# Decays of a two-way state-space scan asked for in four steps between whole tiles, with exponentials held in ScalarE's traced order

## The chip, the cores and the metric

The kernel runs on one core of one Trainium2 chip. The metric is the device time of one execution in microseconds (us), of which the median of several runs is given. The engines are named as in the profile: PE is TensorE's matmuls, PEld its weight loads, DVE is VectorE, ACT is ScalarE, POOL is GpSimd, and SP is SyncE, whose queue issues the kernel's DMA transfers in this stage.

## The reference

One layer of a hybrid network works on 512 latent tokens behind 256 context tokens, each 1024 wide, all in 32-bit floats. One projection of the normalized input feeds a convolution branch (GLU, 31 taps along rows of 64) and a two-way Mamba-2 scan: 32 heads of 64 in 8 groups, a state of 128, chunks of 128 tokens. Both are gated, merged and projected, and an MLP follows. The part that the change is about is the scan's decay inside a chunk:

```python
cum = jnp.cumsum(dts * a.astype(F32).reshape(g, r), axis=2)
xdt = x5 * dts[..., None]
cum_t = jnp.moveaxis(cum, 2, -1)
seg = cum_t[..., :, None] - cum_t[..., None, :]
lower = jnp.tril(jnp.ones((q, q), dtype=bool))
decay = jnp.exp(jnp.where(lower, seg, -jnp.inf))
cb = jnp.einsum('bcqgn,bckgn->bcgqk', cs_, bs)
y_diag = jnp.einsum('bcgrqk,bckgrp->bcqgrp', cb[:, :, :, None] * decay, xdt)
...
y_off = jnp.einsum('bcqgn,bcgrpn,bcqgr->bcqgrp', cs_, h_in, jnp.exp(cum))
return (y_diag + y_off).reshape(b, l, h, p), h_final
```

The scan runs forward and, on the flipped sequence, backward; the two are added.

## The kernel before

**Projections.** Each weight tile comes as fp32 through SP (`raw`, two buffers), is rounded by ACT (`whi`, L115), and DVE takes the rest (`wlo`, L116). PE then does three matmuls for each of eight steps of the contraction, L124 with whi, L125 with whi and the input's low part, L126 with wlo. A B or X tile has a wide part (512 latent tokens) and a narrow one (256 context tokens). A projection needs its own whi and wlo, and they are made one tile ahead.

**The groups.** The time from about 100 to 585 us goes to a loop over the 8 groups. In each round the outputs of group g are computed, and B, C, X0, X1, Z0 and Z1 of group g + 1 are projected. The order of a round is a string, `STEPS` (`STEPS0` for the first round), which the loop reads word by word: a capital B, C, X or Z is a projection, `Gb Ga` the two halves of a GLU tile (Ga is followed by its 31 taps on DVE, L631), `c` makes cb = C'B and the transposes of B (Bk) on PE and copies them on ACT (L503, L510), `x` transposes X (xps), copies it on ACT (xt, L534) and scales it on DVE (xw, L527), `s` makes the chunk states on PE (sps, L546), of which the first is copied by ACT (hst, L552) and the rest added by DVE, and `y0`, `y1` give the outputs of two heads each (L585, L589). cps, bps, xps and sps share three PSUM buffers, so s can be held up by a late copy of xt or of hst. Eviction of a projection is on ACT (L388), its five-tap convolution on DVE (L392), its SiLU on ACT (L402; Z's at L460).

**What sets the order.** PE runs in the order of the string as long as g is under 7. On the other engines a scheduler orders the instructions by the traced order as a priority and by when it expects them ready; each engine then runs its queue strictly in that order.

**The decays.** A head needs two tiles E of 128 x 512, one for each direction. The forward one comes from a ring of 7 buffers, the backward one from a ring of 3. For each: SP fetches a row, broadcast to all partitions (L478); POOL masks one triangle (`affine_select`, L482); ACT takes four exponentials, one for each chunk (L485). DVE adds both (L487) and, in y, multiplies the sum by cb (L575). A backward buffer comes free with the add. All this stands in `expo(upto)`, which traces all four steps for two heads at once, behind the products of each y and two heads ahead of the need (`LEAD` 2). The other rows from the same source, `Cd` (L571), are multiplied by C on POOL or DVE (L572).

Of the kernel before, what the change touches and what calls it, by code (L numbers as in the profile page):

```python
# [27 lines left out]

STEPS0 = 'Gb Ga c0 B x0 C s X0 y0 X1 y1 c Z0 Z1 x'
STEPS = 'B s Gb C X0 y0 Ga X1 y1 c Z0 Z1 x'


CDB, EB, LEAD, ADDV, E_LATER, E_LATER0 = 7, 7, 2, 1, 0, 0


V_N1, V_N2, V_FN = 0, 8, 16
# [28 lines left out]
def build(tc, xT, ctxT, cond, crow, wada1, wada2, vecs, hv, cst, w_in, w_co, w_so, w_o, w_1, w_2, outT):  # L67
    nc = tc.nc
    with ExitStack() as es:
# [393 lines left out]
        def bc(ap, shape):  # L463
            return ap.unsqueeze(len(shape) - 1).broadcast_to(shape)

        ahead = []
        asked = [0]

        def expo(upto):

            while asked[0] < min(upto, HEADS):
                h = asked[0]
                asked[0] += 1
                es_ = []
                for d in range(2):
                    hd = d * HEADS + h
                    e = (tp if d else spool).tile([P, T], F32, name="E", tag="M" if d else "E", bufs=3 if d else EB)
                    nc.sync.dma_start(e, s_cf[hd, 0].unsqueeze(0).broadcast_to([P, T]))  # L478

                    x3 = e.rearrange("p (c q) -> p c q", q=P)  # L480
                    sign = -1 if d else 1
                    nc.gpsimd.affine_select(x3, x3, pattern=[[0, NCH], [sign, P]], compare_op=ALU.is_ge,  # L482
                                            fill=never, base=0, channel_multiplier=-sign)
                    for c in range(NCH):
                        nc.scalar.activation(x3[:, c], x3[:, c], AF.Exp, bias=bT[:, c, hd:hd + 1])  # L485
                    es_.append(e)
                (nc.vector if ADDV else nc.gpsimd).tensor_tensor(es_[0], es_[0], es_[1], ALU.add)  # L487
                ahead.append(es_[0])

        ch = lambda t, c: t[:, c * P:(c + 1) * P]  # L490
        wi = [lambda c: c if c < 3 else c - 1, lambda c: c - 1]
# [70 lines left out]
        def ssd_y(q, j):  # L562
# [4 lines left out]
            for r in range(2):  # L567
                for d in range(2):
                    hd = d * HEADS + 4 * g + 2 * j + r
                    Cd = (spool if d else tp).tile([P, T], F32, name="Cd", tag="Cd", bufs=CDB if d else 3)  # L570
                    nc.sync.dma_start(Cd, s_cf[hd, 1].unsqueeze(0).broadcast_to([P, T]))  # L571
                    (nc.vector if (d, r) in DECAYS_V else nc.gpsimd).tensor_tensor(Cd, Ct, Cd, ALU.mult)  # L572
                    Cs[d].append(Cd)
                M = ahead.pop(0)
                nc.vector.tensor_tensor(M, M, cb, ALU.mult)  # L575
                Ms.append(M)
            with later(E_LATER):
                expo(4 * g + 2 * j + 2 + LEAD)
# [61 lines left out]
        cur = group(0)  # L640
        proj(cur, "Z0")
        proj(cur, "Z1")
        with later(E_LATER0):
            expo(2 + LEAD)
        begun_glu = 0
        for g in range(G):
            nxt = group(g + 1)
            glu_q = None
            for part in STEPS0.split() if g == 0 else STEPS.split():
# [4 lines left out]
                elif part in ("c", "x"):  # L654
                    if g + 1 < G:
                        (ssd_c if part == "c" else ssd_x)(nxt)
                elif part in ("c0", "x0"):
                    (ssd_c if part == "c0" else ssd_x)(cur)
                elif part == "s":
                    ssd_s(cur)  # L660
                elif part[0] == "y":
                    ssd_y(cur, int(part[1]))
                elif part == "Gb":
                    if begun_glu < NGLU:
                        glu_q = glu_b(begun_glu, spool, "sg")
# [290 lines left out]
```

## Time and profile before

| | |
|---|---|
| median of three runs | 1251.92 us (1250.16 to 1253.42) |
| the profiled execution | 1256.71 us |
| its span on the core | 1254.9 us |
| mean granted clock of PE | 0.984 |
| E tiles: rows, masks, exponentials, adds | 64, 64, 256, 32 |
| ACT: mean exponential of 128 x 128 | 394 ns |
| DVE: mean GLU tap | 719 ns |

How to read it: a profile is of one execution, and its own time stands beside its span. A row of a timeline or of a group of instructions has the start or the share, the engine and line, the operation and its tiles (out<-in), and in brackets how long the engine had stood idle ahead of it and who released it. Each engine works its queue in order, so an instruction that waits holds all behind it. Ahead of the groups lie the conditioning and the input's normalization (to about 100 us); behind them three more GLU tiles, the gates, both output projections and the MLP.

### The profile page before, as it was taken

Reading aid. Unit: us, or ns where it says so; the run is one execution under the profiler, and the core shown is the slowest. Engines: PE = TensorE matmul, PEld = TensorE weight load, DVE = VectorE, ACT = ScalarE, POOL = GpSimd, SP = SyncE. Lnnn points to the kernel's source line nnn. Section 1 sums busy time; section 2 is a strip of 40 time slices with the busy share of each in tenths; the row PEclk is TensorE's granted clock in tenths of the full one; section 3 lists DMA queues with packets and bytes.
Section 4 is the critical chain, followed back from the end, with each engine's and each line's share of the span. In section 5 each row is a group of like instructions: output and inputs, shape, how many; then the busy total and the mean of one; then the engine's idle time right before and its main releaser. Section 6 shows DMA issues by size and latency. Waiting matters only on the chain.

```text
span 1254.9 us, 17442 instructions
## 1 busy us (share of the span) xinstructions
PE 1203.4 (96%) x6662; PEld 1005.0 (80%) x6662; DVE 914.7 (73%) x1426; ACT 598.4 (48%) x941; POOL 156.7 (12%) x138
## 2 busy tenths in 40 slices
PE   6998899999999989999999999999999999999997
PEld 3787778878787878887887878778988888888886
DVE  6797899988989799875999698786843443443454
ACT  4567786847557475842452561134531331332342
POOL 0003523323050314130010000000000000000000
PEclk8999899999999999999999999999999999999998
DMA  9427544425352434333353368855113223323332
GB/s 362 142 61 200 176 138 143 147 79 170 96 190 73 155 113 142 108 118 110 102 186 115 126 201 274 309 164 160 54 56 101 89 96 101 100 86 101 101 101 68
DMA packets 65332, 169.83 MB, mean 135 GB/s; under 512 B 7648, under 2 KB 10464, under 8 KB 65120
## 3 DMA queue, kind: packets, MB, share of 16 engines
q1 hardware_dynamic: 65248, 168.72, 42.3%
q8 instruction: 52, 0.85, 0.3%
q14 instruction: 32, 0.26, 0.1%
HBM read 162.14 MB, written 6.55 MB: 134 GB/s over the span
## 4 chain that ended last, share of the span: by engine, by line
PE 48%; DVE 6%; DMA 6%; ACT 2%; issue 1%; SPq 0%; POOL 0%; DVEq 0%; ACTq 0%; POOLq 0%
PE ps L125 15%; PE ps L126 15%; PE ps L124 15%; DMA aw<-in_wada_dram 2%; DVE conv L631 1%; DVE wlo L116 1%; DMA yr<-s_y 1%; PE yps L589 1%; DMA raw<-in_w_dram 1%; DVE aw L755 1%; DMA raw<-in_w_co_dram 1%; DVE yl L694 1%; DMA raw<-in_w_o_dram 1%; PE sps L546 1%; ACT whi L115 0%
## 5 line engine op out<-in xcount | busy, mean ns | idle before, releaser
L115 ACT CAST whi<-raw 128x1024 fp32r<-128x1024 f32 x163 | 170.9, 1049 | 333.2 <-PE ps L125 314.2
L116 DVE TENSOR_TENSOR wlo<-raw,whi 128x1024 fp32r<-128x1024 f32 x163 | 202.1, 1241 | 105.1 <-ACT whi L115 96.8
L126 PE MATMUL ps<-hh,wlo 128*128 128x512 f32 x632 | 248.5, 393 | 7.8 <-DVE wlo L116 7.8
L124 PE MATMUL ps<-hh,whi 128*128 128x512 f32 x632 | 252.8, 400 | 0.6 <-DVE Bt L392 0.4
L125 PE MATMUL ps<-hl,whi 128*128 128x512 f32 x632 | 247.9, 392 | 0.0
L631 DVE SCALAR_TENSOR_TENSOR conv<-sg,V,conv 128x392 f32<-128x392 f32 (+14 forms) x240 | 168.6, 719 | 2.6
L126 PEld LDWEIGHTS ps<-hh,wlo 128*128 128x128 f32 x632 | 119.3, 189 | 35.7 <-DVE wlo L116 10.3
L124 PEld LDWEIGHTS ps<-hh,whi 128*128 128x128 f32 x632 | 120.0, 190 | 27.0 <-issue 2.4
L125 PEld LDWEIGHTS ps<-hl,whi 128*128 128x128 f32 x632 | 119.8, 189 | 24.8 <-issue 0.6
L791 DVE SCALAR_TENSOR_TENSOR x<-ps,mod,x 128x512 f32<-128x512 f32 (+1 forms) x48 | 31.7, 661 | 99.5 <-PE ps L126 99.5
L485 ACT ACTIVATE E<-E,bT 128x128 f32<-128x128 f32 x256 | 84.0, 394 | 31.0 <-POOL E L482 30.4
L125 PE MATMUL ps<-h2l,whi 128*128 128x512 f32 (+1 forms) x240 | 89.9, 375 | 0.1
L126 PE MATMUL ps<-h2h,wlo 128*128 128x512 f32 (+1 forms) x240 | 89.8, 375 | 0.0
L124 PE MATMUL ps<-h2h,whi 128*128 128x512 f32 (+1 forms) x240 | 89.4, 375 | 0.0
L125 PE MATMUL ps<-gl,whi 128*128 128x512 f32 x224 | 88.4, 395 | 0.0
L124 PE MATMUL ps<-gh,whi 128*128 128x512 f32 x224 | 88.2, 394 | 0.0
L126 PE MATMUL ps<-gh,wlo 128*128 128x512 f32 x224 | 87.9, 392 | 0.0
L572 POOL TENSOR_TENSOR Cd<-Ct,Cd 128x512 f32<-128x512 f32 x48 | 71.2, 1503 | 96.0 <-ACT Ct L402 49.7
L482 POOL TENSOR_SCALAR_AFFINE_SELECT E<-E 128x512 f32<-128x512 f32 x64 | 51.4, 812 | 251.1 <-DMA E<-s_cf 203.8
L392 DVE SCALAR_TENSOR_TENSOR Xt<-ps,V,Xt 128x255 f32<-128x255 f32 (+3 forms) x128 | 75.3, 608 | 9.1 <-ACT Xt L388 8.3
L546 PE MATMUL sps<-xw,Bk 128*128 128x256 f32 x160 | 42.1, 415 | 12.8 <-ACT hst L552 8.8
L124 PE MATMUL ps<-hc,whi 128*128 128x256 f32 x184 | 52.0, 283 | 1.4 <-DVE Xt L392 1.4
(260 smaller groups left out, 2327.5 us busy)
## 6 DMA issues: line engine op xcount, KB each, us to landing
raw<-in_w_in_dram SPq DMA_DIRECT2D x81, 512.0 KB, 3.7
raw<-in_w_dram SPq DMA_DIRECT2D x64, 512.0 KB, 3.6
E<-s_cf SPq DMA_DIRECT2D x64, 256.0 KB, 4.5
Cd<-s_cf SPq DMA_DIRECT2D x64, 256.0 KB, 4.4
aw<-in_wada_dram SPq DMA_DIRECT2D x64, 256.0 KB, 4.2
ablk<-in_wada_dram SPq DMA_DIRECT2D x16, 512.0 KB, 8.9
raw<-in_w_so_dram SPq DMA_DIRECT2D x16, 512.0 KB, 3.8
s_y<-yt SPq DMA_DIRECT2D x16, 256.0 KB, 3.6
```

The costliest lines, as they stand in the source:

```text
L115: nc.scalar.copy(hi, raw)
L116: nc.vector.tensor_tensor(lo, raw, hi, ALU.subtract)
L124: pe(nc.tensor.matmul(ps, lhsT=whi[:, k, :], rhs=rhi[:, k, t0:t1], start=start and k == 0, stop=False))
L125: pe(nc.tensor.matmul(ps, lhsT=whi[:, k, :], rhs=rlo[:, k, t0:t1], start=False, stop=False))
L126: pe(nc.tensor.matmul(ps, lhsT=wlo[:, k, :], rhs=rhi[:, k, t0:t1], start=False, stop=stop and k == KT - 1))
L392: nc.vector.scalar_tensor_tensor(o[:, lo:hi], ps[:, lo + d:hi + d], vcol(V_SCW + 5 * ch + j), o[:, lo:hi], ALU.mult, ALU.add)
L482: nc.gpsimd.affine_select(x3, x3, pattern=[[0, NCH], [sign, P]], compare_op=ALU.is_ge, fill=never, base=0, channel_multiplier=-sign)
L485: nc.scalar.activation(x3[:, c], x3[:, c], AF.Exp, bias=bT[:, c, hd:hd + 1])
L546: pe(nc.tensor.matmul(ps[:, d * 256:(d + 1) * 256], lhsT=ch(Bk, c), rhs=xw[d][:, wi[d](c)].rearrange("p h e -> p (h e)"), start=i == 0, st ...
L572: (nc.vector if (d, r) in DECAYS_V else nc.gpsimd).tensor_tensor(Cd, Ct, Cd, ALU.mult)
L631: nc.vector.scalar_tensor_tensor(o[:, :, lo:hi], u[:, :, lo + d:hi + d], wv(j), o[:, :, lo:hi], ALU.mult, ALU.add)
L791: nc.vector.scalar_tensor_tensor(x1[:, j, a:b], ps[:, a:b], mod[:, gcol + j, 0:1], x1[:, j, a:b], ALU.mult, ALU.add)
```

## The change

1. `expo` is taken apart into `expo_rows` (SP), `expo_select` (POOL), `expo_exp` (ACT) and `expo_add` (DVE). A word `e` in the string calls `expo()`, which advances one head: the add for the head 2 ahead, the exponentials 3 ahead, the mask 4 ahead, the rows 5 ahead (`LEADS`). A word `E` in the first round primes them (`expo_first`).
2. The first of the four exponentials of each tile is passed to the scheduler's `keep_in_program_order`, which puts it behind the ACT instruction traced just before it.
3. The strings change: four `e` in each round, one between two whole tiles. In the first round C and X0 come ahead of s, and a second GLU tile is done there; in the later rounds both halves of the GLU tile stand together, ahead of X0. Five tiles in all are done in the groups as before: two in round 0 and one each in rounds 1 to 3, in place of one each in rounds 0 to 4.

The diff's core:

```diff
-STEPS0 = 'Gb Ga c0 B x0 C s X0 y0 X1 y1 c Z0 Z1 x'
-STEPS = 'B s Gb C X0 y0 Ga X1 y1 c Z0 Z1 x'
-CDB, EB, LEAD, ADDV, E_LATER, E_LATER0 = 7, 7, 2, 1, 0, 0
+STEPS0 = 'Gb Ga c0 B x0 C X0 s E e X1 e y0 e Gb Ga y1 e c Z0 Z1 x'
+STEPS = 'B s e C e Gb Ga X0 y0 e X1 e y1 c Z0 Z1 x'
+LEADS = (2, 3, 4, 5)
...
+        def after_traced(ins):
+            tc.keep_in_program_order(ins)
...
+        def expo_exp(h):
+            for d in range(2):
+                hd = d * HEADS + h
+                e3 = chain[d][h].rearrange("p (c q) -> p c q", q=P)
+                for c in range(NCH):
+                    i = nc.scalar.activation(e3[:, c], e3[:, c], AF.Exp, bias=bT[:, c, hd:hd + 1])
+                    if c == 0:
+                        after_traced(i)
...
+        def expo_first():
+            for h in range(LEADS[3]):
+                expo_rows(h)
+            for h in range(LEADS[2]):
+                expo_select(h)
+            for h in range(LEADS[1]):
+                expo_exp(h)
+            for h in range(LEADS[0]):
+                expo_add(h)
+
+        def expo():
+            n = step[0]
+            step[0] += 1
+            for lead, f in zip(LEADS, (expo_add, expo_exp, expo_select, expo_rows)):
+                if 0 <= n + lead < HEADS:
+                    f(n + lead)
...
-                M = ahead.pop(0)
+                M = chain[0][4 * g + 2 * j + r]
                 nc.vector.tensor_tensor(M, M, cb, ALU.mult)
                 Ms.append(M)
-            with later(E_LATER):
-                expo(4 * g + 2 * j + 2 + LEAD)
...
-        with later(E_LATER0):
-            expo(2 + LEAD)
...
+                elif part == "e":
+                    expo()
+                elif part == "E":
+                    expo_first()
```

The code grows by 27 lines, so the lines behind it have other numbers in after: cb's copy is L530, Bk's L537, xt's L561, hst's L579, the exponentials L491, the add L497, the product with cb L602, the taps L656.

How the queues move shows at four places. First ACT in the first round, before: from the end of a long run of exponentials (E) to the copies of cb and Bk.

```order
L388 ACTIVATE Bt_1106<-ps_1107,V_72 128x512 [waits PE_49]
L485 ACTIVATE E_962<-E_962,bT_572 128x128
L485 ACTIVATE E_970<-E_970,bT_572 128x128 [waits DMAHW4_49,Pool_49]
L485 ACTIVATE E_970<-E_970,bT_572 128x128 x3
L485 ACTIVATE E_977<-E_977,bT_572 128x128 [waits DMAHW2_49,Pool_49]
L485 ACTIVATE E_977<-E_977,bT_572 128x128
L388 ACTIVATE Bt_1106<-ps_1137,V_72 128x256 [waits PE_49]
L115 CAST whi_1256<-raw_1254 128x1024 [waits DMAHW0_49]
L485 ACTIVATE E_977<-E_977,bT_572 128x128 x2
L503 COPY cb_1087<-cps_1082 128x512
L510 COPY Bk_1089<-bps_1090 128x512
L510 COPY Bk_1089<-bps_1096 128x256
```

The same stretch of ACT after, from the first of these copies on.

```order
L376 COPY bT_572<-dtp_791 128x64
L650 ACTIVATE conv_717<-sg_956,V_72 128x512 [waits DVE_49]
L530 COPY cb_1027<-cps_1022 128x512 [waits PE_49]
L537 COPY Bk_1029<-bps_1030 128x512 [waits PE_49]
L537 COPY Bk_1029<-bps_1036 128x256 [waits PE_49]
L491 ACT_TABLE_LOAD [waits DMAHW5_49,Activation_49]
L491 ACTIVATE E_1262<-E_1262,bT_572 128x128 [waits Pool_49]
L491 ACTIVATE E_1262<-E_1262,bT_572 128x128
L491 ACTIVATE E_1262<-E_1262,bT_572 128x128 [waits Activation_49]
L491 ACTIVATE E_1264<-E_1264,bT_572 128x128 [waits DMAHW6_49,Pool_49]
L491 ACTIVATE E_1264<-E_1264,bT_572 128x128 x3
```

The copies of cb and Bk have moved from behind the exponentials to ahead of all of them.

Second, ACT in the same round after, around the copy hst of the first state (Ct_1140 and Xt_1178 are C and X0 of the next group, whi_1475 is a rounded weight).

```order
L491 ACTIVATE E_1327<-E_1327,bT_572 128x128 [waits DMAHW7_49]
L388 ACTIVATE Xt_1178<-ps_1179,V_72 128x512 [waits PE_49]
L491 ACTIVATE E_1327<-E_1327,bT_572 128x128 x2
L491 ACTIVATE E_1410<-E_1410,bT_572 128x128 [waits DMAHW0_49]
L491 ACTIVATE E_1410<-E_1410,bT_572 128x128
L402 ACT_TABLE_LOAD [waits DVE_49]
L402 ACTIVATE Ct_1140<-Ct_1140 128x512 [waits Activation_49]
L388 ACTIVATE Xt_1178<-ps_1209,V_72 128x256 [waits PE_49]
L115 CAST whi_1475<-raw_1473 128x1024 [waits DMAHW0_49]
L579 COPY hst_1240<-sps_1241 128x512 [waits PE_49]
```

Before, hst stood directly behind the second copy of xt; after, a SiLU with its table load, an eviction and a rounding stand ahead of it.

Third, DVE between rounds 0 and 1, after: the end of the stretch between the wlo of the B projected at the start of round 1 (wlo_1744, seven rows ahead of the first row here) and the add that frees the buffer of E_1844.

```order
L656 SCALAR_TENSOR_TENSOR conv_717<-sg_956,V_72,conv_717 128x8x49 [waits DVE_49]
L554 TENSOR_TENSOR xw0_1716<-xps_1718,wgT_573 128x512 [waits PE_49]
L116 TENSOR_TENSOR wlo_1849<-raw_1846,whi_1848 128x1024 [waits DMAHW6_49,Activation_49]
L554 TENSOR_TENSOR xw1_1717<-xps_1718,wgT_573 128x512
L554 TENSOR_TENSOR xw0_1716<-xps_1725,wgT_573 128x512 [waits PE_49]
L554 TENSOR_TENSOR xw1_1717<-xps_1725,wgT_573 128x256
L554 TENSOR_TENSOR xw0_1716<-xps_1733,wgT_573 128x256 [waits PE_49]
L554 TENSOR_TENSOR xw1_1717<-xps_1733,wgT_573 128x512
L656 SCALAR_TENSOR_TENSOR conv_717<-sg_1504,V_72,conv_717 128x8x54 [waits DVE_49]
L497 TENSOR_TENSOR E_1327<-E_1327,E_1329 128x512 [waits Activation_49]
```

The same place before, from just ahead of the wlo of that B (wlo_1623) on.

```order
L631 SCALAR_TENSOR_TENSOR conv_717<-sg_1016,V_72,conv_717 128x8x61 [waits DVE_49]
L487 TENSOR_TENSOR E_1879<-E_1879,E_1886 128x512 [waits DMAHW5_49,DMAHW1_49,Pool_49]
L631 SCALAR_TENSOR_TENSOR conv_717<-sg_1016,V_72,conv_717 128x8x62 [waits DVE_49]
L116 TENSOR_TENSOR wlo_1623<-raw_1620,whi_1622 128x1024 [waits DMAHW7_49,PE_49,Activation_49]
L631 SCALAR_TENSOR_TENSOR conv_717<-sg_1016,V_72,conv_717 128x8x63 [waits DVE_49]
L575 TENSOR_TENSOR E_1864<-E_1864,cb_1515 128x512
L631 SCALAR_TENSOR_TENSOR conv_717<-sg_1016,V_72,conv_717 128x8x63 [waits DVE_49]
L116 TENSOR_TENSOR wlo_1713<-raw_1710,whi_1712 128x1024 [waits DMAHW2_49,PE_49,Activation_49]
L527 TENSOR_TENSOR xw0_1595<-xps_1597,wgT_573 128x512 [waits PE_49]
L527 TENSOR_TENSOR xw1_1596<-xps_1597,wgT_573 128x512
```

Before, the last add of the round (E_1879) stood ahead of that wlo; after, E_1327's stands behind taps of two GLU tiles and all six scalings xw, and on ACT the first exponential of E_1844 stands ahead of hst:

```order
L561 COPY xt_1715<-xps_1725 128x512 [waits DVE_49,PE_49]
L561 COPY xt_1715<-xps_1733 128x512 [waits DVE_49,PE_49]
L388 ACTIVATE Bt_1747<-ps_1748,V_72 128x512 [waits PE_49]
L491 ACTIVATE E_1844<-E_1844,bT_572 128x128 [waits DMAHW7_49,Pool_49]
L388 ACTIVATE Bt_1747<-ps_1778,V_72 128x256 [waits PE_49]
L115 CAST whi_1901<-raw_1899 128x1024 [waits DMAHW5_49,Activation_49]
L491 ACTIVATE E_1844<-E_1844,bT_572 128x128 x2
L579 COPY hst_1809<-sps_1810 128x512 [waits PE_49]
L491 ACTIVATE E_1469<-E_1469,bT_572 128x128
L491 ACTIVATE E_1844<-E_1844,bT_572 128x128
```

Fourth, ACT at the start of the round that computes group 2's states, before.

```order
L485 ACTIVATE E_3110<-E_3110,bT_572 128x128 [waits Pool_49]
L534 COPY xt_2217<-xps_2227 128x512 [waits DVE_49,PE_49]
L485 ACTIVATE E_3110<-E_3110,bT_572 128x128
L534 COPY xt_2217<-xps_2235 128x512 [waits DVE_49,PE_49]
L485 ACTIVATE E_3110<-E_3110,bT_572 128x128 x2
L388 ACTIVATE Bt_2249<-ps_2250,V_72 128x512 [waits PE_49]
L485 ACTIVATE E_3325<-E_3325,bT_572 128x128 [waits DMAHW2_49,Pool_49]
L388 ACTIVATE Bt_2249<-ps_2280,V_72 128x256 [waits PE_49]
L115 CAST whi_2368<-raw_2366 128x1024 [waits DMAHW0_49,Activation_49]
L485 ACTIVATE E_3325<-E_3325,bT_572 128x128
L552 COPY hst_2311<-sps_2312 128x512 [waits PE_49]
```

The same after.

```order
L561 COPY xt_2338<-xps_2348 128x512 [waits DVE_49,PE_49]
L491 ACTIVATE E_2467<-E_2467,bT_572 128x128 [waits DMAHW7_49,Pool_49]
L561 COPY xt_2338<-xps_2356 128x512 [waits DVE_49,PE_49]
L491 ACTIVATE E_2467<-E_2467,bT_572 128x128 x3
L491 ACTIVATE E_2518<-E_2518,bT_572 128x128 [waits DMAHW2_49]
L388 ACTIVATE Bt_2370<-ps_2371,V_72 128x512 [waits PE_49]
L491 ACTIVATE E_2518<-E_2518,bT_572 128x128 x2
L115 CAST whi_2524<-raw_2522 128x1024 [waits DMAHW0_49,PE_49,Activation_49]
L388 ACTIVATE Bt_2370<-ps_2401,V_72 128x256 [waits PE_49]
L579 COPY hst_2432<-sps_2433 128x512 [waits PE_49]
```

The exponentials that wait for POOL (E_3325 before, E_2467 after) stood between the evictions of B and hst and now stand ahead of the evictions, between the two copies of xt.

More of the change, by code (lines that the diff above doesn't have):

```diff
@@ L27 @@
 NEVER, DT_MIN = -1e30, 1e-18
-STEPS0 = 'Gb Ga c0 B x0 C s X0 y0 X1 y1 c Z0 Z1 x'
-STEPS = 'B s Gb C X0 y0 Ga X1 y1 c Z0 Z1 x'
-CDB, EB, LEAD, ADDV, E_LATER, E_LATER0 = 7, 7, 2, 1, 0, 0
+STEPS0 = 'Gb Ga c0 B x0 C X0 s E e X1 e y0 e Gb Ga y1 e c Z0 Z1 x'
+STEPS = 'B s e C e Gb Ga X0 y0 e X1 e y1 c Z0 Z1 x'
+LEADS = (2, 3, 4, 5)
+CDB, EB = 7, 7
 V_N1, V_N2, V_FN = 0, 8, 16
@@ L464, in bc @@
             return ap.unsqueeze(len(shape) - 1).broadcast_to(shape)
[L466 to L488, printed above, removed]
+        chain = [[None] * HEADS for _ in range(2)]
@@ new lines, in build, with expo_rows, expo_select @@
+        step = [0]
+        def after_traced(ins):
+            tc.keep_in_program_order(ins)
+        def expo_rows(h):
+            for d in range(2):
+                e = (tp if d else spool).tile([P, T], F32, name="E", tag="M" if d else "E", bufs=3 if d else EB)
+                nc.sync.dma_start(e, s_cf[d * HEADS + h, 0].unsqueeze(0).broadcast_to([P, T]))
+                chain[d][h] = e
+        def expo_select(h):
+            for d in range(2):
+                e3 = chain[d][h].rearrange("p (c q) -> p c q", q=P)
+                sign = -1 if d else 1
+                nc.gpsimd.affine_select(e3, e3, pattern=[[0, NCH], [sign, P]], compare_op=ALU.is_ge,
+                                        fill=never, base=0, channel_multiplier=-sign)
@@ new lines, in expo_exp, with expo_add @@
+        def expo_exp(h):
+            for d in range(2):
+                hd = d * HEADS + h
+                e3 = chain[d][h].rearrange("p (c q) -> p c q", q=P)
+                for c in range(NCH):
+                    i = nc.scalar.activation(e3[:, c], e3[:, c], AF.Exp, bias=bT[:, c, hd:hd + 1])
+                    if c == 0:
+                        after_traced(i)
+        def expo_add(h):
+            f, b = chain[0][h], chain[1][h]
+            nc.vector.tensor_tensor(f, f, b, ALU.add)
```

## The prediction

> **What bounds the kernel now.** I read the page's first two parts, then the chain of waits of TensorE (PE), then the windows for the granted clock, and last the timelines of PE and ScalarE (ACT) at the places that those named.
>
> ```profile
> PE 1203.4 (96%) x6662; PEld 1005.0 (80%) x6662; DVE 914.7 (73%) x1426; ACT 598.4 (48%) x941; POOL 156.7 (12%) x138
> PE ps L126 <- DVE wlo L116: 10.5, 9, 2.4
> PE sps L546 <- ACT hst L552: 8.8, 5, 2.5
> PE sps L546 <- ACT xt L534: 4.0, 1, 4.0
> PE xps L522 <- ACT cb L503: 4.0, 1, 4.0
> ```
>
> PE works 1203.4 of 1254.9 us. Its matmuls are the same in number and shape after the change, so only its 51.5 idle us, and what the clock loses, can be won. The four rows (us waited, times, longest) hold 27.3 us of the idle time. Three of them name a copy on ACT, though ACT is busy for only 48%. So ACT is not slow but stands still at the wrong moment:
>
> ```profile
> 104.76 6.84 ACT L485 ACTIVATE E<-E,bT 128x128 f32<-128x128 f32 x23
> 116.19 0.57 ACT L503 COPY cb<-cps 128x512 f32<-128x512 f32 x1
> 129.91 0.40 ACT L485 ACTIVATE E<-E,bT 128x128 f32<-128x128 f32 x1 [3.20 <-POOL E L482]
> 130.21 0.56 ACT L534 COPY xt<-xps 128x512 f32<-128x512 f32 x1
> 253.80 0.40 ACT L485 ACTIVATE E<-E,bT 128x128 f32<-128x128 f32 x1 [4.02 <-POOL E L482]
> 255.79 0.57 ACT L552 COPY hst<-sps 128x512 f32<-128x512 f32 x1
> ```
>
> In group 0 a run of 23 exponentials, and more behind it, stands ahead of cb. At 129.91 and 253.80 one exponential waits 3.20 and 4.02 us for its masked row E, and xt or hst, which PE needs, stands behind it in ACT's queue. What PE then lost:
>
> ```profile
> 116.81 2.82 PE L522 MATMUL xps<-C,Xt 128*128 128x128 f32 x12 [3.95 <-ACT cb L503]
> 130.83 5.88 PE L546 MATMUL sps<-xw,Bk 128*128 128x256 f32 x12 [3.96 <-ACT xt L534]
> 187.34 1.13 PE L546 MATMUL sps<-xw,Bk 128*128 128x256 f32 x4 [1.73 <-ACT hst L552]
> 256.41 2.07 PE L546 MATMUL sps<-xw,Bk 128*128 128x256 f32 x4 [2.45 <-ACT hst L552]
> 314.66 0.50 PE L126 MATMUL ps<-hh,wlo 128*128 128x512 f32 x1 [2.42 <-DVE wlo L116]
> 384.41 0.50 PE L126 MATMUL ps<-hh,wlo 128*128 128x512 f32 x1 [2.09 <-DVE wlo L116]
> 453.25 0.50 PE L126 MATMUL ps<-hh,wlo 128*128 128x512 f32 x1 [1.53 <-DVE wlo L116]
> ```
>
> Four matmuls last 2.07 us behind the gap at 256.41 and 1.13 behind that at 187.34: the clock is cut after some gaps. The windows around the cuts (the seventh entry is the granted clock):
>
> ```profile
> 116.00:120.00 4.00, 3.19 (x15) 3.11 (x16) 4.00 (x8) 3.10 (x7) 0.00 (x0) 0.57 0.69 197
> 129.00:137.00 8.00, 6.14 (x14) 4.48 (x15) 5.51 (x8) 7.09 (x19) 3.81 (x7) 0.57 0.38 120
> 256.00:260.00 4.00, 3.59 (x9) 2.89 (x10) 4.00 (x8) 3.31 (x8) 0.00 (x0) 0.57 0.39 111
> 385.00:390.00 5.00, 5.00 (x16) 3.97 (x15) 5.00 (x10) 3.82 (x7) 0.00 (x0) 0.66 0.65 208
> 467.00:472.00 5.00, 4.63 (x13) 3.71 (x14) 5.00 (x9) 3.35 (x8) 0.00 (x0) 0.66 0.36 105
> ```
>
> Length by what is missing to 1.00: 4 x 0.43 = 1.7, 8 x 0.43 = 3.4, 1.7, 5 x 0.34 = 1.7 and 1.7, together 10.2 us. So the waits that the change can reach cost about 27 + 10 = 37 us.
>
> **The change part by part.** The same decays are computed by the same instructions; what changes is when they are asked for, and the place of two GLU tiles. The one addition is table loads: ACT switches between exponentials and SiLU more often, 97 loads in the order of after against 76.
>
> ```profile
> L485 ACT ACT_TABLE_LOAD x31 | 39.8, 1283 | 22.1 <-DMA E<-s_cf 21.7
> L402 ACT ACT_TABLE_LOAD x19 | 24.4, 1283 | 22.6 <-DVE Xt L392 12.4 <-DVE Bt L392 9.9 <-issue 0.3
> 119.12 1.28 ACT L402 ACT_TABLE_LOAD   x1 [0.90 <-DVE Bt L392]
> 120.42 0.85 ACT L402 ACTIVATE Bt<-Bt 128x768 f32<-128x768 f32 x1
> ```
>
> 21 x 1.283 = 27 us more on ACT. I cost them at nothing: ACT would be busy 625 of 1255 us, and a load before a SiLU passes while ACT waits for DVE anyway (12.4 and 9.9 us in the second row). If that cover fails, each is 1.3 us. [...]
>
> The "hold" binds less than its name. In the order of after only the first of four exponentials of a forward row is pinned behind the instruction traced before it; the backward row's first is pinned behind the forward row's fourth, which is itself free. So 32 of 256 are held, and the others still float to where the scheduler expects them to be ready.
>
> *Group 0.* In after cb and Bk stand ahead of the first exponential, and C and X0 come on PE between the transposes x0 and the states s, so that s doesn't meet an xt just queued. Gone: 3.95 + 3.96 us and the clock of the first two windows, 1.7 + 3.4: 13.0. New: hst now stands last in the row SiLU load, SiLU of Ct, Xt's eviction, whi, hst. These last about 1.28 + 0.85 + 0.55 + 1.05 + 0.57 = 4.3 us from the moment that DVE's Ct is ready, against PE's sixteen matmuls of s ahead of the wait (3.61 us, below) if both start together. Between nothing and 4.3 + 1.7 of clock; I take 3.3 + 1.7, near the upper end, since DVE has 11 more GLU taps in group 0. Net -13.0 + 5.0 = **-8.0 us**.
>
> *Group 1.* Here the change loses. PE's next need is hst after B's projection and sixteen matmuls:
>
> ```profile
> 182.00 3.61 PE L546 MATMUL sps<-xw,Bk 128*128 128x256 f32 x16
> 119.74 0.39 PE L125 MATMUL ps<-hl,whi 128*128 128x512 f32 x1
> 124.75 0.40 PE L126 MATMUL ps<-hh,wlo 128*128 128x512 f32 x1
> 109.83 0.28 PE L124 MATMUL ps<-hc,whi 128*128 128x256 f32 x1
> 112.58 0.28 PE L126 MATMUL ps<-hc,wlo 128*128 128x256 f32 x1
> 309.11 4.36 DVE L631 SCALAR_TENSOR_TENSOR conv<-sg,V,conv 128x440 f32<-128x440 f32 x6
> 313.38 1.22 DVE L116 TENSOR_TENSOR wlo<-raw,whi 128x1024 fp32r<-128x1024 f32 x1
> 315.93 1.28 DVE L527 TENSOR_TENSOR xw<-xps,wgT 128x512 f32<-128x512 f32 x2
> L482 POOL TENSOR_SCALAR_AFFINE_SELECT E<-E 128x512 f32<-128x512 f32 x64 | 51.4, 812 | 251.1 <-DMA E<-s_cf 203.8
> E<-s_cf SPq DMA_DIRECT2D x64, 256.0 KB, 4.5
> ```
>
> A wide matmul comes every 5.01/22 = 0.23 us, a narrow one every 2.75/23 = 0.12, so B takes 24 x (0.23 + 0.12) = 8.4 us, and hst is wanted 8.4 + 3.6 = 12.0 us after B's wlo. On ACT it stands behind the first exponential of E_1844, whose buffer is free only after the add E_1327. That add stands on DVE eight taps, one further wlo and six xw behind B's wlo: 8 x 0.73 + 1.2 + 6 x 0.64 = 10.9 us. Then come the add (0.7), the row's transfer (4.5), the select (0.7 alone, 0.8 on average) and the exponential (0.4): 17.2 us. hst is 17.2 - 12.0 = 5 us late; I take 4.5, since taps and xw overlap a little. That is past every gap that cut the clock, so 1.7 more; before had 1.73. B's wlo itself stands behind seventeen taps of two GLU tiles; before's two wlo waits of over 2 us had six taps ahead. I take 1.3 us, between 0 and 2.4. Net 4.5 + 1.7 - 1.7 + 1.3 = **+5.8 us**.
>
> *Groups 2 to 6, hst.* In after the add that frees the late row's buffer stands ahead of B's wlo, by two taps, a product with cb and the wlo itself. From its start the masked exponential is ready after 0.7 + 4.5 + 0.7 + 0.4 = 6.3 us; B's wlo ends some 4.1 us after that start, and PE then has 8.4 us of B left before s asks for xt, and 12.0 before it asks for hst. So the slack is 4.1 + 8.4 - 6.3 = 6.2 us, and nothing that waits for a row stands between B's evictions and hst. Of the 8.8 - 1.7 = 7.1 us of hst waits in these groups I leave 1.5. Two of the five clock cuts, behind 256.41 and 467, go: 3.4. Net **-9.0 us**.
>
> *Groups 2 to 6, wlo.* Both halves of the GLU tile move ahead of X0, so between the two outputs stands X1 alone, and the products M for y1 no longer heap up ahead of B's wlo beside the taps. The three waits at 314, 384 and 453 are 6.0 us. DVE has as much to do as before, and the row at 314 shows what one late operand costs; I leave 3.5 and the one clock cut (385). Net **-2.5 us**; between -6.0 and +4.
>
> *The rest.* SyncE (SP) issues all rows, Cd loads and weights in one queue, so a row that waits for its buffer holds the weights behind it. A weight load lands in about as long as a row, and both raw buffers are loaded a tile ahead; I cost it at nothing, with +3 as the bound. The stages after the groups keep their order, and their waits are small.
>
> Sum: -8.0 + 5.8 - 9.0 - 2.5 = **-13.7 us**. The profiled run took 1256.71 us (span 1254.9), 4.8 above the median of the three runs, 1251.92. From the profiled run it gives 1243; from the median 1251.9 - 13.7 = **1238.2 us**.
>
> [...]
>
> **The rivals.**
>
> *The late row in every group (slower).* Group 1's chain could be the rule: if the add lands over 6.2 us later than walked, each of groups 2 to 6 waits as group 1 does. Price: six waits of 4.5 + 1.7 = 37.2 us in place of 8.8 + 3.4, with group 0's gain and wlo as it is: 37.2 - 12.2 - 8.0 = +17.0, 1269 us; in half of the groups about +5, 1257. For it: 203.8 us in the row L482 above, POOL's wait for rows. Against it: DVE's order in groups 2 to 6. Chance 0.15.
>
> *The loads on the path (slower).* If all 21 loads stood where PE waits, 21 x 1.283 = 27 less 13.7 is +13, 1265 us; seven, one a group, leave 9.0 - 13.7 = -4.7, 1247. For it: in after a SiLU load stands ahead of hst in group 0. Against it: in the later groups they stand behind hst. Chance 0.05 for the first; the second lies within my range. [...]
>
> *The hold binds too little (no change).* The free exponentials block ACT as before: groups 2 to 6 keep their waits, group 0 gives 8.0 and group 1 takes 5.8: -2.2, 1249.7 us. For it: 32 of 256. Against it: in groups 2 to 6 the blocking one has moved ahead of B's evictions. Chance 0.13.
>
> **How the numbers follow.** My forecast has 0.67. About 0.3%, 3.7 us, is what a measurement of this kernel can tell from no change. The forecast's own range is 1238 -8 (wlo at -6.0, group 0's new wait at nothing) to +11 (wlo at +4, SP at +3, hst in two groups kept), 1230 to 1249. To hold 8 in 10 it takes in the no-change rival and reaches nearly to the late row in half of the groups: 1229 to 1256. Faster: 0.67 and a quarter of the no-change rival, 0.70; same 0.11; slower 0.19.
>
> **What would show it.** Right: PE's waits for cb and xt in group 0 gone, one hst wait of 4 to 5 us in group 1, hst of groups 2 to 6 under 2 us in sum, PE idle near 40 us, Exp loads near 42. Wrong: an hst or xt wait in each group with the exponential ahead of it waiting for POOL (the late row); ACT rows of loads just ahead of hst or whi while PE waits (the loads); wlo over 10 us in sum (DVE's order).

## The result and the profile after

The changed kernel takes 1261.49 us in the median of 8 runs (1256.79 to 1264.44), the kernel before 1252.36 us (8 runs, 1250.16 to 1254.09): a ratio of 1.0073, 95% interval 1.0052 to 1.0093. It is slower by 9 us; I had forecast 13.7 us less. The profiled execution took 1257.76 us, one of the shorter ones, and before's, 1256.71, was longer than those eight, so the two profiles differ by 1 us alone. They have to be compared by stage.

The page of after, then PE's chain of waits (us in total, times, longest):

```profile
PE 1204.4 (96%) x6662; PEld 1005.7 (80%) x6662; DVE 927.4 (74%) x1426; ACT 627.7 (50%) x962; POOL 165.2 (13%) x138
```

```profile
PE sps L573 <- ACT hst L579: 8.2, 2, 5.7
PE ps L124 <- DVE Bt L392: 6.5, 2, 6.1
PE ps L124 <- ACT whi L115: 6.0, 2, 3.1
PE ps L126 <- DVE wlo L116: 5.4, 7, 2.3
```

The waits for cb and xt (8.0 us) are gone, the five for hst have become two, those for wlo have halved from 10.5 to 5.4. PE's idle time, for which I had named 40 us, is 51.6 (1256.0 less 1204.4). In place of the waits that went stand two names that before's list did not have in the groups: Bt, 6.1 us at once, and whi, 6.0 us in two waits. Where on PE's timeline the longest lie:

```profile
124.07 0.77 PE L124 MATMUL ps<-hh,whi 128*128 128x512 f32 x1 [6.08 <-DVE Bt L392]
...
200.36 1.22 PE L573 MATMUL sps<-xw,Bk 128*128 128x256 f32 x2 [5.73 <-ACT hst L579]
...
332.92 0.80 PE L124 MATMUL ps<-hh,whi 128*128 128x512 f32 x1 [3.14 <-ACT whi L115]
```

The granted clock around three of the five, from the windows (the entry behind the five engines); it is 0.57 at 260 to 268 and at 332 to 340 as well:

```profile
120.00:128.00 8.00, 3.69 (x8) 2.53 (x9) 7.90 (x14) 6.92 (x21) 6.95 (x7) 0.57 0.77 241
141.00:145.00 4.00, 4.00 (x12) 3.19 (x11) 4.00 (x6) 3.55 (x10) 4.00 (x3) 0.57 0.34 76
199.00:207.00 8.00, 6.64 (x17) 5.29 (x18) 8.00 (x14) 4.03 (x8) 0.08 (x1) 0.57 0.36 98
```

Four long cuts of 8 us and a short one of 4 (at 141), 0.43 x 36 = 15.5 us, against 10.2 before.

For the sum I take the group stage, from PE's first transposes of dt (L371) to the end of its last output matmul. It lasts 484.3 us in before's profile and 489.3 in after's. PE's idle time in it went from 25.7 to 27.4 us, the clock's loss from 10.2 to 15.4; what is left, work at the full clock, is 448.3 and 446.6. So after's group stage lost 6.8 us to waits and clock and the rest gave 1.8 back. The stage behind the groups was 3.6 us shorter (671.0 and 667.4), which is why the two profiles look alike.

**The wait for Bt.** The first exponentials of after, in ACT's timeline, and the chain of waits at that place (start, length, what was waited for):

```profile
111.57 1.28 ACT L491 ACT_TABLE_LOAD   x1 [7.85 <-DMA E<-s_cf]
...
118.07 0.40 ACT L491 ACTIVATE E<-E,bT 128x128 f32<-128x128 f32 x1 [0.87 <-POOL E L483]
118.37 0.76 ACT L388 ACTIVATE Bt<-ps,V 128x512 f32<-128x512 f32 x1
```

```profile
100.73 14.46 DMA E<-s_cf
```

SP's queue in before, and in after, where the first rows were issued:

```profile
97.18 1.31 SPq L478 DMA_DIRECT2D E<-s_cf  x3
```

```profile
98.41 1.34 SPq L366 DMA_DIRECT2D s_dec<-dec  x3
99.85 1.31 SPq L476 DMA_DIRECT2D E<-s_cf  x3
...
DMA to landing us min/median/max: 3.0/4.2/14.5
```

Before issued its first rows at 97.18 us, ahead of the small transfers of the chunk decays (s_dec). After issued them at 99.85, right behind these, and the third took 14.46 us to land, where the median of all rows is 4.2. ACT, which had been through with cb and Bk, stood idle for 7.85 us, then began on the exponentials, and B's eviction, which PE needed, had to wait for twelve of them.

**The waits for whi.** The end of round 3: DVE's last tap of X1, then ACT:

```profile
323.16 0.47 DVE L392 SCALAR_TENSOR_TENSOR Xt<-ps,V,Xt 128x254 f32<-128x254 f32 x1
325.75 0.40 ACT L491 ACTIVATE E<-E,bT 128x128 f32<-128x128 f32 x1 [1.61 <-POOL E L483]
326.17 1.28 ACT L402 ACT_TABLE_LOAD   x1
...
328.33 1.28 ACT L491 ACT_TABLE_LOAD   x1
329.62 0.40 ACT L491 ACTIVATE E<-E,bT 128x128 f32<-128x128 f32 x1
330.04 1.28 ACT L460 ACT_TABLE_LOAD   x1
...
331.83 1.04 ACT L115 CAST whi<-raw 128x1024 fp32r<-128x1024 f32 x1
```

Three loads of 1.28 us stand ahead of the whi that PE waits for, and two of them are there for one exponential of 0.40 us. But before has the same three loads around one exponential at this place:

```profile
304.12 1.28 ACT L402 ACT_TABLE_LOAD   x1 [2.49 <-DVE Xt L392]
...
306.81 1.28 ACT L485 ACT_TABLE_LOAD   x1
308.10 0.40 ACT L485 ACTIVATE E<-E,bT 128x128 f32<-128x128 f32 x1
308.52 1.28 ACT L460 ACT_TABLE_LOAD   x1
...
310.31 1.04 ACT L115 CAST whi<-raw 128x1024 fp32r<-128x1024 f32 x1
```

So the row of loads is not new. New is what stands ahead of it: X1 was ready at 323.63, yet its SiLU's load began 2.5 us later, behind an exponential that waited 1.61 us for POOL's mask. In before that load began as soon as X1 was ready. From X1's last tap to the end of this whi ACT took 9.2 us in after and 7.3 in before. At the end of round 2 it is the same (X1 ready at 250.76, the load at 253.13, an exponential that waited 1.17 us for POOL between them).

The exponentials of after float apart. ACT's order shows a forward tile in two pieces, three exponentials and, some 40 rows further on, the fourth (E_1262 is head 0's, hst_1240 the copy of the first state):

```
95 L491 ACTIVATE E_1262<-E_1262,bT_572 128x128 [waits Pool_49]
...
97 L491 ACTIVATE E_1262<-E_1262,bT_572 128x128 [waits Activation_49]
...
133 L579 COPY hst_1240<-sps_1241 128x512 [waits PE_49]
134 L491 ACT_TABLE_LOAD
135 L491 ACTIVATE E_1262<-E_1262,bT_572 128x128
```

The priming is traced behind s. The held exponential stays behind it; the three free ones run ahead to where the row is expected. Counted over ACT's order, this is so in all 32 forward tiles of after: the held exponential comes last, and ten or more other ACT instructions lie between the first and the last of the four. In before no tile is spread so far. The exponentials at 252.71 and 325.75, which hold up X1's SiLU, are free ones of such tiles. One late piece makes the whole tile late: the add has to wait for it, and with the add the buffer of a later row.

### The profile page after: what moved, and what is told of

Read it like the earlier page. It is cut to its first block, busy times and chain, and to the rows that moved or that the text cites. A ratio compares the mean times of both kernels' runs of the same rounds, so it can differ in the third digit from the quotient of the medians.

```text
span 1256.0 us, 17441 instructions
## 1 busy us (share of the span) xinstructions
PE 1204.4 (96%) x6662; PEld 1005.7 (80%) x6662; DVE 927.4 (74%) x1426; ACT 627.7 (50%) x962; POOL 165.2 (13%) x138
## 4 chain that ended last, share of the span: by engine, by line
PE 59%; DVE 21%; DMA 9%; ACT 6%; issue 4%; POOL 1%; SPq 1%; DVEq 0%; ACTq 0%; POOLq 0%
PE ps L124 18%; PE ps L126 18%; PE ps L125 18%; DVE conv L656 6%; DVE wlo L116 3%; DMA aw<-in_wada_dram 2%; DMA E<-s_cf 2%; DVE Xt L392 2%; PE sps L573 1%; DMA Cd<-s_cf 1%; DMA yr<-s_y 1%; PE yps L614 1%; ACT whi L115 1%; DVE Bt L392 1%; DMA raw<-in_w_dram 1%
## 5 line engine op out<-in xcount | busy, mean ns | idle before, releaser
L124 PE MATMUL ps<-hh,whi 128*128 128x512 f32 x632 | 255.5, 404 | 12.9 <-DVE Bt L392 6.5
L126 PE MATMUL ps<-hh,wlo 128*128 128x512 f32 x632 | 251.5, 398 | 5.2 <-DVE wlo L116 5.1
L656 DVE SCALAR_TENSOR_TENSOR conv<-sg,V,conv 128x392 f32<-128x392 f32 (+14 forms) x240 | 175.8, 757 | 3.1 <-ACT conv L650 0.7
L491 ACT ACTIVATE E<-E,bT 128x128 f32<-128x128 f32 x256 | 85.6, 394 | 51.8 <-POOL E L483 51.2
L483 POOL TENSOR_SCALAR_AFFINE_SELECT E<-E 128x512 f32<-128x512 f32 x64 | 55.5, 877 | 302.5 <-DMA E<-s_cf 262.7
L392 DVE SCALAR_TENSOR_TENSOR Xt<-ps,V,Xt 128x254 f32<-128x254 f32 (+3 forms) x128 | 74.7, 607 | 11.6 <-ACT Xt L388 11.0
```

The source lines that it names most:

```text
L124: pe(nc.tensor.matmul(ps, lhsT=whi[:, k, :], rhs=rhi[:, k, t0:t1], start=start and k == 0, stop=False))
L126: pe(nc.tensor.matmul(ps, lhsT=wlo[:, k, :], rhs=rhi[:, k, t0:t1], start=False, stop=stop and k == KT - 1))
L392: nc.vector.scalar_tensor_tensor(o[:, lo:hi], ps[:, lo + d:hi + d], vcol(V_SCW + 5 * ch + j), o[:, lo:hi], ALU.mult, ALU.add)
L483: nc.gpsimd.affine_select(e3, e3, pattern=[[0, NCH], [sign, P]], compare_op=ALU.is_ge, fill=never, base=0, channel_multiplier=-sign)
L491: i = nc.scalar.activation(e3[:, c], e3[:, c], AF.Exp, bias=bT[:, c, hd:hd + 1])
L656: nc.vector.scalar_tensor_tensor(o[:, :, lo:hi], u[:, :, lo + d:hi + d], wv(j), o[:, :, lo:hi], ALU.mult, ALU.add)
```

## The experiments

Ratios are to the kernel before, run on the same chip, with the 95% interval; differences between two experiments go by their ratios (0.1% is 1.25 us).

**Rows asked for early.**

```diff
         def expo_first():
-            for h in range(LEADS[3]):
-                expo_rows(h)
...
+        for h in range(LEADS[3]):
+            expo_rows(h)
         begun_glu = 0
```

> After, with only the rows of the first five heads asked for ahead of the loop; masks, exponentials and adds are primed where they were. In after these rows stand on SP behind the four transfers of the chunk decays, the first exponential starts at 111.6 us and PE waits 6.08 us at 124 us for DVE's Bt. Theory A (the late rows cost what after lost in the first round): that wait goes, with some 2 us of clock, so 6 to 9 us less than after's 1261.5, near 1254. Theory B (the table loads of the held exponentials): no change, 1261 +- 2.

Measured: 1260.05 us, 1.0062 (1.0041 to 1.0082). PE's waits:

```profile
PE ps L124 <- ACT whi L115: 8.9, 7, 2.9
PE sps L571 <- ACT hst L577: 8.7, 1, 8.7
```

The wait for Bt went, as theory A said, and the time barely moved: a single wait for hst of 8.71 us at 142 took its place, since ACT then stood for 5.15 and 3.03 us at exponentials whose mask wasn't done. So the late rows made the wait for Bt, but they are not what made after slower: without them the same floating exponentials hold up hst.

**No hold.**

```diff
                     i = nc.scalar.activation(e3[:, c], e3[:, c], AF.Exp, bias=bT[:, c, hd:hd + 1])
-                    if c == 0:
-                        after_traced(i)
```

> After, with no exponential held in the traced order; all else is the same. The order has 72 table loads in place of 97. Theory B (lone held exponentials put three table loads ahead of whi, at the ends of rounds 2 and 3): the waits for whi of 2.89 and 3.14 us, 1.24 us of wlo behind the first and some 6 us of clock go, 1248 to 1252. Theory A: the wait of 6.08 us for Bt stays and so does the time, 1260 +- 2.

Measured: 1266.34 us, 1.0111 (1.0089 to 1.0132), slower than after. Both theories fall.

```profile
PE sps L571 <- ACT hst L577: 17.4, 6, 4.8
...
PE ps L124 <- DVE Bt L392: 6.1, 2, 5.7
```

Without a hold the loads were fewer (72), and hst was waited for in six rounds; at 194.79, 342.24 and 414.73 ACT has an exponential that waits 0.55 to 1.04 us for POOL just ahead of it. So the hold does what the change says, as far as it goes: it takes 9 us of hst waits away.

**Almost no table loads in the groups, after and before.** These two kernels leave out the SiLU of B, C, X and Z.

```diff
-            nc.scalar.activation(o, o, AF.Silu)
+            nc.scalar.activation(o, o, AF.Identity)
...
-                    nc.scalar.activation(z, ps, AF.Silu)
+                    nc.scalar.activation(z, ps, AF.Identity)
```

> After, with the SiLU of B, C, X and Z in the groups left out (an identity stands in its place, so that no table has to be changed there). The order has 15 table loads in place of 97. Theory B: the waits for whi go and the kernel is 8 to 14 us faster than after, 1248 to 1253, and ends no later than before with the same thing left out. Theory A: it gains only what before gains by it and stays some 9 us behind that.

> Before, with the SiLU of B, C, X and Z in the groups left out in the same way; 15 table loads in place of 76. Theory B says that before's loads were mostly covered: 1246 to 1252. If the loads of before stood on the path as well, it gains 5 us or more and the comparison with after has to be made between these two alone.

Measured: after so 1258.22 us, 1.0052 (1.0037 to 1.0067); before so 1244.89, 0.9937 (0.9917 to 0.9956). The loads of before cost 0.6%, 8 us, those of after 0.2%, 3 us, and with nearly all loads gone (15 left in all of each kernel) after is 1.15%, 14 us, behind. So the 21 more loads are not what makes after slower; whi is waited for (5.4 us) without them too, the longest time behind exponentials that wait for POOL:

```profile
PE ps L124 <- ACT whi L115: 5.4, 3, 3.3
```

```profile
452.76 1.86 ACT L491 ACTIVATE E<-E,bT 128x128 f32<-128x128 f32 x6 [3.26 <-POOL E L483]
454.52 1.03 ACT L115 CAST whi<-raw 128x1024 fp32r<-128x1024 f32 x1
```

(The scheduler places instructions anew where no load is due, so this says what loads cost in sum, not at one place.)

**One GLU tile a round.**

```diff
-STEPS0 = 'Gb Ga c0 B x0 C X0 s E e X1 e y0 e Gb Ga y1 e c Z0 Z1 x'
+STEPS0 = 'Gb Ga c0 B x0 C X0 s E e X1 e y0 e y1 e c Z0 Z1 x'
```

> After, with the second GLU tile of the first round taken out, so that rounds 0 to 4 do one GLU tile each as in before. Theory C (two tiles' taps on VectorE hold back the add that frees the late row): the wait of 5.73 us for hst in round 1 falls under 2 us and its half-clock stretch goes, 1252 to 1256. Theory D (the decays asked for one at a time and late are what costs): the waits for whi and wlo of the later rounds stay and round 4 gets one more, 1259 to 1264.

Measured: 1261.08 us, 1.008 (1.0057 to 1.0103). The wait in round 1 was still 5.00 us, and hst was waited for in four later rounds by 1.7 to 2.9. Theory C falls: the taps of the second tile are not what held the row back. (The edit also brings a wait of its own, 4.74 us at 156.71 for Cd, with y1 directly behind y0.)

**The new steps in the old order.**

```diff
-STEPS0 = 'Gb Ga c0 B x0 C X0 s E e X1 e y0 e Gb Ga y1 e c Z0 Z1 x'
-STEPS = 'B s e C e Gb Ga X0 y0 e X1 e y1 c Z0 Z1 x'
+STEPS0 = 'E Gb Ga c0 B x0 C s X0 y0 e e X1 y1 e e c Z0 Z1 x'
+STEPS = 'B s Gb C X0 y0 e e Ga X1 y1 e e c Z0 Z1 x'
```

> After's four functions, leads and hold, in the order of before: priming at the head of the first round, two steps behind each y, GLU halves, C, X0 and s where before has them. 81 table loads. Theory D (steps between whole tiles): with the steps back behind the outputs it is like before, 1248 to 1254. Theory E (the leads themselves, a mask and a row that wait for the add three heads on): hst waits return in every round and it is slower than after, over 1262.

Measured: 1278.85 us, 1.0226 (1.0203 to 1.0249). No rise of hst; one wait of 26.73 us in round 0 and one of 7.44 in round 7:

```profile
179.94 1.34 PE L610 MATMUL yps<-E,xt 128*64 128x128 f32 x10 [26.73 <-DVE E L602]
```

ACT ahead of it:

```profile
175.49 0.62 ACT L659 COPY cacc<-conv 128x512 f32<-128x512 f32 x1 [12.79 <-DVE conv L656]
176.01 0.62 ACT L622 ACTIVATE yacc<-yt 128x512 f32<-128x512 f32 x1
176.64 1.28 ACT L491 ACT_TABLE_LOAD   x1
177.94 0.40 ACT L491 ACTIVATE E<-E,bT 128x128 f32<-128x128 f32 x1
```

The held exponential stands behind yacc, which was traced just ahead of it (in y0), and yacc behind a copy that waits 12.79 us for the GLU tile's taps. The time is over theory E's 1262, but without the hst waits that it named, so this decides between neither. It shows the hold's price: a held instruction inherits the waits of what stands ahead of it, 12.79 us here.

**The new order with the old expo.**

```diff
-STEPS0 = 'Gb Ga c0 B x0 C s X0 y0 X1 y1 c Z0 Z1 x'
-STEPS = 'B s Gb C X0 y0 Ga X1 y1 c Z0 Z1 x'
+STEPS0 = 'Gb Ga c0 B x0 C X0 s X1 y0 Gb Ga y1 c Z0 Z1 x'
+STEPS = 'B s C Gb Ga X0 y0 X1 y1 c Z0 Z1 x'
```

> Before's expo and its lead of two heads, with the orders of after: C and X0 ahead of s in the first round, two GLU tiles in it, both GLU halves ahead of X0 in the later ones. 78 table loads. Theory C (the orders cost it): 1257 or more, with a wait for hst in round 1 of 4 us or more. Theory D (the chain costs it, the orders help): the waits for cb stay, that for xt goes, 1244 to 1250.

Measured: 1260.16 us, 1.007 (1.0049 to 1.009). The order alone costs 9 us, with the exponentials as free as before:

```profile
PE sps L546 <- ACT hst L552: 10.7, 4, 4.6
...
PE ps L124 <- ACT whi L115: 6.8, 4, 3.4
```

Theory C named the wait (hst, 4.62 us in round 0 and 3.42 in round 1, where it said 4 or more), if not its reason. Of theory D the wait for xt went and that for cb stayed, but the time refutes that the order helps. The waits for whi come with the order too: at the end of round 3 here 2.10 us for whi and 2.42 for wlo, though X1's SiLU is not held up (its load begins as X1 is ready). How much of after's whi waits is the order's and how much the free exponential's, no run here parts.

**All four held.**

```diff
                     i = nc.scalar.activation(e3[:, c], e3[:, c], AF.Exp, bias=bT[:, c, hd:hd + 1])
-                    if c == 0:
-                        after_traced(i)
+                    after_traced(i)
```

> After, with all four exponentials of a tile held in the traced order instead of the first. 82 table loads in place of 97. If lone exponentials between two SiLUs cost after its waits for whi, these go and it gains 4 to 8 us, 1253 to 1257. If the held ones stand ahead of evictions until their row is there, waits for Bt and hst come in each round, 1265 or more.

Measured: 1249.16 us, 0.9991 (0.9977 to 1.0005): 0.8%, 10 us less than after by one condition taken out, and level with before. No tile is spread over ten instructions any more.

```profile
PE yps L609 <- DVE E L601: 7.5, 1, 7.5
...
PE sps L572 <- ACT hst L578: 3.4, 2, 3.0
```

The long wait for Bt is gone, those for hst are down to 3.4 us, whi has one of 1.57 left over 0.5 (at the end of round 3, with the same three loads ahead of it). What is left is one wait of 7.5 us, y0 of the first round for its own product: now all primed exponentials stand behind s.

**A second and a third profile of after, a second one of before.** No edit.

> The changed kernel itself, a second profile. Its eight times spread from 1256.8 to 1264.4 and the first profile is of one of the short ones. All theories: the same waits in the first two rounds (Bt near 6, hst near 2.5 and 5.7 us) and at the ends of rounds 2 and 3; in the late stage more waits for wlo than the 4.5 us of idle time there in the first profile.

> The kernel before, a second profile. Its first one, 1256.7 us, lies over all its timed runs. If the group stage varies, it is some 480 us here against 484.3; if the stages around vary, 484 again with a shorter late stage. The waits of the group stage are the same ones: cb and xt near 4 us, hst near 2 in most rounds, wlo near 2 at the ends of rounds 2 to 4.

> The changed kernel, a third profile. The group stage again between 486 and 492 us with the waits for Bt, hst and whi of the first two profiles; a time over 1260 would show which stage makes the long executions long.

Measured: after 1256.07 and 1263.44 us, before 1252.66. The group stage was 486.7 and 494.1 us in after (489.3 in the first profile) and 481.2 in before (484.3). The means are 490.0 and 482.7, 7.3 apart. The stage behind the groups was shorter in all three profiles of after (667.4 to 669.5) than in both of before (671.0 and 671.9), by 2.7 us in the mean, so these five executions differ by 4.4 us in all where the medians differ by 9.1: the loss lies in the group stage, and its whole size is not in the profiles. The longest execution, 1263.44, was long in the group stage (494.1, over the 486 to 492 expected), where the clock cost 17.1 us against 11.9 in the shortest. After had the same waits in all three profiles: Bt 5.6 to 6.1, hst of round 1 4.8 to 5.7, whi 2.8 to 3.1 at the ends of rounds 2 and 3. The stages ahead and behind vary by 1 to 2 us from one execution to the next, in both kernels.

**All held, and primed earlier.** The first of these adds the early rows (the diff of the first experiment) to the kernel with all held; the second moves the priming too:

```diff
-STEPS0 = 'Gb Ga c0 B x0 C X0 s E e X1 e y0 e Gb Ga y1 e c Z0 Z1 x'
+STEPS0 = 'Gb Ga c0 E B x0 C X0 s e X1 e y0 e Gb Ga y1 e c Z0 Z1 x'
```

> All four exponentials held, and the first rows asked for ahead of the loop. With all held, y0 of the first round waits 7.50 us for its product, which starts from rows that land late. Theory F (the rows): that wait falls to 2 us or less and its half-clock stretch with it, 1238 to 1243. Theory G (the held exponentials themselves, which stand behind hst): the wait stays, 1247 to 1251.

> As the last, and the priming (masks, exponentials, adds) moved from behind s to directly behind cb and Bk of the first round. Theory G: the wait of y0 goes, the first exponentials stand in the idle time of ScalarE ahead of B's evictions, 1236 to 1242. Theory F: no better than with the rows alone. If they stand ahead of the evictions too long, a wait for Bt of 3 us or more comes back.

Measured: 1244.24 us, 0.9939 (0.9917 to 0.9961), and 1236.55 us, 0.9883 (0.9855 to 0.9911). The rows alone leave the wait of y0 where it was (8.92 us, so theory G, though the time lies between the ranges of both theories: the kernel is 0.5% faster by the wait for hst, 0.64 in place of 3.00, and the clock, 5.1 in place of 10.2 lost):

```profile
150.83 1.09 PE L607 MATMUL yps<-E,xt 128*64 128x128 f32 x7 [8.92 <-DVE E L599]
```

With the priming directly behind cb and Bk it goes. PE's wait for hst in the faster one, the longest that is left in one piece:

```profile
PE sps L570 <- ACT hst L576: 4.7, 3, 2.8
```

Its group stage is 466.7 us, with 15.3 idle and 1.7 lost to the clock. It beats both kernels, after by 1.9%, 24 us, and before by 1.2%, 15 us.

**Before with the hold alone.**

```diff
-                        nc.scalar.activation(x3[:, c], x3[:, c], AF.Exp, bias=bT[:, c, hd:hd + 1])
+                        tc.keep_in_program_order(nc.scalar.activation(x3[:, c], x3[:, c], AF.Exp, bias=bT[:, c, hd:hd + 1]))
```

> Before, with every exponential held in the traced order; nothing else. 63 table loads in place of 76. If the hold is what the whole change needed, it gains without the new steps: hst waits of 8.8 us fall to 3 or less, 1240 to 1246. If the steps are needed to give each held exponential its place, eight tiles' exponentials stand in one block ahead of evictions and it is slower than before, 1255 or more.

Measured: 1251.22 us, 0.9994 (0.9977 to 1.0012), neither. The hst waits over 0.5 us are all gone and so is most of xt's, and the outputs wait in their place, in two rounds. Ahead of the longest wait the sixteen exponentials of two heads stood on ACT together (472.36 to 479.20); that this is why they came too late is my reading:

```profile
PE yps L585 <- DVE E L575: 12.5, 3, 8.3
```

## Why the prediction was wrong

What happened in each step, in us of PE's idle time and clock, first profile of after against the profile of before:

| step | forecast | measured |
|---|---|---|
| group 0: cb, xt and their clock gone | -13.0 | -13.0 |
| group 0: new wait for hst, with clock | +5.0 | +4.2 (2.50 + 1.7) |
| group 0: wait for Bt, with clock | none | +9.5 (6.08 + 3.4) |
| group 1: hst, B's wlo | +5.8 | +7.4 (5.73 + 3.4 - 1.73) |
| groups 2 to 6: hst, with clock | -9.0 | -10.5 (none left) |
| groups 2 to 6: wlo, and now whi, with clock | -2.5 | +8.4 |
| small ones | 0 | +0.8 |
| sum | -13.7 | +6.8 |

The row of wlo and whi: wlo went from 6.65 (0.61 + 2.42 + 2.09 + 1.53) to 3.9, as forecast, but whi added 2.89 + 3.14, and the clock 5.1 (two cuts of 3.4 in place of one of 1.7).

**Right:** the waits that would go, the new one in group 0, the late row in group 1 and its price (5.73 for 4.5), the hst waits of groups 2 to 6, and that their wlo waits would nearly halve. The price of the late row was right partly by luck. In the trace the exponential ended 14.9 us after B's wlo where I had 17.2, and an eviction, whi, two more exponentials and hst itself, 2.5 us that I had not counted, followed. Nor was the reason all of it: with half of the taps taken away (one GLU tile a round) 5.00 us were left.

**Wrong, the step "In after cb and Bk stand ahead of the first exponential".** I took the copies' gain and gave the exponentials no new price: +9.5 us. They were moved behind cb, and their rows were moved too, on SP behind the transfers of the chunk decays; I walked ACT's queue and not SP's, on which a row needed 14.46 us.

**Wrong, the step "I leave 3.5 and the one clock cut (385)", the wlo of groups 2 to 6.** It walked DVE alone. The wlo waits fell as it said, but whi, which it gave no wait at all, took 6.03 us and two long cuts of the clock: +8.4 for -2.5. In those groups I had followed ACT from B's evictions to hst and not at the end of the round, where a free exponential that waits for its mask stands ahead of X1's SiLU, and so of whi.

**The loads.** The step "I cost them at nothing" is not what failed. Three loads do stand in a row ahead of whi while PE waits, the sign that I had named for that rival, but before has the same row, and after is 14 us behind before when neither has more than 15 loads. In the rows at 328.33 and 329.62 a load lasts 1.28 us, and the exponential starts 1.29 us behind the start of its load, the 1.3 us that I had set for a load without cover.

The rival of the late row in every group comes nearest in the kernel without a hold (17.4 us in six waits for hst); after has it in round 1 alone.

**The cause that both steps missed** stood in my own text: "So 32 of 256 are held, and the others still float". I read this as a hold too weak to matter. It is worse than weak. The held exponential keeps its place and its three companions leave it, so the three stand early where others wait for ACT (Bt, X1's SiLU ahead of whi) and the one comes late and alone (the add, the row). The runs in a line show what this costs, as ratios to before: nothing held 1.0111, the first of four held 1.0073, all held 0.9991, and 0.9883 with the rows and the priming earlier as well. The half hold gains 0.4% of the 1.2% that the whole one gains.

**The order, too, has a price.** With the old expo the new order of PE costs 9 us (1260.2), as much as the whole change does, where I had credited it with the waits for xt and wlo. So the loss against before can't be put down to the half hold alone; that holding the other three takes 10 us away is what is shown. What the new order takes in itself, without floating exponentials, no run shows apart; with all held and primed early it is part of the fastest kernel. That no part tried by itself gains (order alone +9 us, hold alone within 0.2% of before) and all together, primed early, gain 15 is shown; which of the parts the fastest could do without is open.

The price of the clock: a wait of 2.50 us (141) was followed by a short cut here as well, so the forecast's 1.7 us held there. The four longer ones cost 3.4 each in this profile. Both sizes stood in the windows of before, and I priced all new ones at the small one.

## What to carry to other kernels

A hint that pins one instruction of a group that belongs together split the group in all 32 forward tiles here: pin all of it or none, and count in the new order how far its pieces lie apart before pricing anything else. Where an operation is moved, walk the queue of its transfer as well as its own. A wait for a copy on an engine that is half idle (ACT was busy for 48% in before and 50% in after) is a matter of what stands ahead of it, and removing that only helps if what replaces it has its operands by then. And a row of instructions ahead of a wait explains it only if the kernel before, which did not wait there, hasn't the same row.

## What the runs showed of the hardware

Rows of 256 KB that land in 4.2 us in the median took up to 14.46 us behind four small transfers: the 0.1 KB writes of s_dec themselves took 8.3 us in the median, twice as long as transfers of two thousand times their size. From 102 to 108 us, with three rows and a weight issued, the DMA engines were busy for 0.03 of the time; the last small transfer landed at 107.68 and the first row at 111.48.

```profile
s_dec<-dec SPq DMA_DIRECT2D x3, 0.1 KB, 8.3
```

The clock's cuts were not set by the length of the wait alone: before's waits of 2.42 and 2.45 us were followed by no cut and by one, and its two in the first round, 3.95 and 3.96 us, by 4 x 0.43 and 8 x 0.43. In the traces of before and after the cuts go with how PE's idle time lies in time. Each of the two records 15 changes of the clock, between 1.00 and 0.50, and within a trace all 15 lie on one grid with steps of 3.41 us, to 0.01 us. Of the steps at the full clock between 60 and 800 us (416 in the two traces), all 10 with 2.00 us or more of idle time on PE are followed by a step at half the clock (0.50), and none of the 406 with 1.90 us or less is. Of the 15 steps at half the clock, the four with 0.97 us or more of idle time are followed by another, and the nine with 0.30 us or less are not; of the two between, the one with 0.45 us is and the one with 0.64 us is not. These are counts from two executions, not thresholds. Before's steps, with PE's busy time as the second entry:

```profile
252.70:256.11 3.41, 1.26 (x6) 0.76 (x4) 2.34 (x5) 2.31 (x5) 1.27 (x2) 1.00 0.07 25
310.73:314.14 3.41, 1.51 (x12) 1.08 (x10) 3.30 (x5) 3.36 (x6) 0.00 (x0) 1.00 0.00 0
116.17:119.58 3.41, 2.77 (x13) 2.77 (x14) 3.41 (x7) 2.52 (x6) 0.00 (x0) 0.50 0.66 190
129.82:133.23 3.41, 2.37 (x5) 1.47 (x6) 1.74 (x2) 3.33 (x6) 2.98 (x6) 0.50 0.39 146
```

Of the 2.45 us 2.15 lay in one step, and the next was cut; of the 2.42 us 1.90, and it was not. Behind the 3.95 us the half-clock step had 0.64 us of idle time and stayed alone; behind the 3.96 us it had 1.04, and a second followed.
